# Seven products for eight: the second feed-forward product by Strassen's scheme, with the weights' sums on GpSimd

## The chip, the cores and the metric

The kernel runs on one NeuronCore of a Trainium2 chip. Its time is device microseconds for one execution of the whole program. TensorE (PE) multiplies and writes only into PSUM (eight banks of 128 x 512 float32); VectorE (DVE), ScalarE (ACT) and GpSimd (POOL) work on SBUF; DVE and ACT also read PSUM; SyncE (SP) issues the DMA loads. Each engine runs its own instructions strictly in order, and the engines wait for each other by semaphores.

## The reference

Two decoder blocks on 512 tokens of width 1024, in float32. All that matters here is the end of the second block: the feed-forward layer and the last norm.

```
    h = h + merged @ w_out[l]
    hn = rmsnorm(h, norm2_g[l])
    h = h + jnp.square(jax.nn.relu(hn @ w_ff1[l])) @ w_ff2[l]
return rmsnorm(h, final_g)
```

`w_ff1` is 1024 x 4096 and `w_ff2` is 4096 x 1024.

## The kernel before

**Products in three passes.** A float32 matrix is kept as two float32r parts, `hi` (a rounded copy, made by ACT) and `lo` (the rest, made by a DVE subtraction of two SBUF operands): `split`, line 516. `mm3` (line 559) multiplies hi x hi, hi x lo and lo x hi into one PSUM bank. So each 128 x 128 by 128 x 512 step is three matmuls of 512 columns.

**The feed-forward stage** starts at line 1465. The 4096 hidden columns go by in four quarters (`q`, line 1468), and each quarter has two products:

- The first product makes eight tiles of 128 hidden columns by 512 tokens (`dense_T`, 24 matmuls each). `unit` loads 512 KB of `w_ff1` into a `w_raw` buffer and splits it into one of three `w_hi`/`w_lo` pairs. ACT applies Relu, DVE squares, and `split` writes the tile into `HB` (hi and lo).
- The second product multiplies `HB` (stationary, tokens as columns) by 1024 rows of `w_ff2` (moving), in two halves of 512 output columns: `dense_N`, four units of 24 matmuls per half. That is 8 units and 192 matmuls a quarter. `ev_ff` adds each of the eight result tiles (4 token tiles x 2 column halves) to `x16`, the residual, with one DVE addition that reads PSUM.
- In the last quarter `out_proj` goes by token halves, so that the norm of the first tokens is done while the rest is multiplied. It keeps four of the split units in free places of `KR` and `HA` and loads the other four twice (12 units). Then square (ACT), `rstd` (one small DVE operation and a power on POOL), scaling and the store of a tile.

**The order.** The program is recorded and then laid out by a planner (`Recorder.schedule`, line 198) that works with written-down costs and gives each engine a fixed order, with the more urgent of the ready operations first. It counts an SBUF operation of POOL with two operands at 2.1 ns an element and 100 ns, and it lets no engine slow another. All instructions are issued from line 274, so the profile tells groups apart by their tiles: `bank` is PSUM, `arena` the shared scratch tile, `sp` small column vectors, `sq` the norm's scratch. Buffers are handed out in the order of the program text: a third use of a `w_hi` buffer in turn waits for the matmuls of the first.

Of the kernel before, what the change touches and what calls it, by code (L numbers as in the profile page):

```python
# [29 lines left out]
AF = mybir.ActivationFunctionType  # L30
OP = mybir.AluOpType
# [248 lines left out]
T = 512  # L280
D = 1024
# [126 lines left out]
def body(ctx: ExitStack, tc: tile.TileContext, x, norm_pre_w, norm_post_w, positions, norm1_g, norm2_g, final_g,  # L408
# [4 lines left out]
    v, s, g, pe, sy = (rec.engine(n) for n in ("vector", "scalar", "gpsimd", "tensor", "sync"))  # L413
# [4 lines left out]
    def tiles(n, bufs, name, dt=F32, p=pool):  # L418
        return Ring([p.tile([128, n], dt, name=f"{name}{i}") for i in range(bufs)])

    w_raw, w_hi, w_lo = tiles(1024, 2, "w_raw"), tiles(1024, 3, "w_hi", F32R), tiles(1024, 3, "w_lo", F32R)
    HA = [pool.tile([128, 8, T], F32R, name=f"ha{i}") for i in range(2)]
    HB = [pool.tile([128, 8, T], F32R, name=f"hb{i}") for i in range(2)]
    KR = pool.tile([128, 8, T], F32R, name="kr")
    x16 = pool.tile([128, NT, D], F32, name="x16")
    sqr = tiles(1024, 1, "sq")
    tmp = Ring([sqr.tiles[0][:, i * T:(i + 1) * T] for i in range(2)])
    ar = Arena(pool.tile([128, ARENA], F32, name="arena"), ARENA)
    bank = [pp.tile([128, T], F32, name=f"bank{i}") for i in range(8)]
    dn = Ring(bank[:4])  # L430
# [7 lines left out]
    def small(n=4):  # L438
        return sp_ring(128, n)

    x2 = x[0]
    w_in, w_out, w_in2, w_br_a, w_br_b, w_out2, w_ff1, w_ff2, cmp_w1_k, cmp_w1_v = packed

    def bcast(row, n):
        return bass.AP(tensor=row.tensor, offset=row.offset, ap=[[0, 128], [1, n]])
# [7 lines left out]
    def tt(e, o, a, b, op):  # L453
        e.tensor_tensor(o, a, b, op)
# [4 lines left out]
    def strided(t, off, *dims):  # L459
        return bass.AP(tensor=t.tensor, offset=t.offset + off, ap=[list(t.ap[0])] + [list(d) for d in dims])  # L460
# [5 lines left out]
    def norm_weight(dst, row):  # L466
        sy.dma_start(dst, bcast(row, D))
        return dst[:, :512], dst[:, 512:]
# [37 lines left out]
    def rstd(ss):  # L506
        r = small(1)
        v.scalar_tensor_tensor(r, ss[:, 0:1], EPS, ss[:, 1:2], op0=OP.add, op1=OP.add)
        tt(g, r, r, mhalf[:, :1], OP.pow)
        return r  # L510
# [5 lines left out]
    def split(hi, lo, src, scale=None, e=v):  # L516
        if scale is None:
            s.activation(hi, src, AF.Copy)
            tt(e, lo, src, hi.bitcast(F32), OP.subtract)
        else:  # L520
            s.activation(hi, src, AF.Copy, scale=scale)
            v.scalar_tensor_tensor(lo, src, scale, hi.bitcast(F32), op0=OP.mult, op1=OP.subtract)

    def square(t, c, ss, e=None):

        cs = slice(c * 512, c * 512 + 512)
        if e is not None:
            e.tensor_tensor_reduce(tmp(128, T), x16[:, t, cs], x16[:, t, cs], 1.0 / D, 0.0, OP.mult, OP.add,
                                   ss[:, c:c + 1])
            return  # L530
        s.activation(tmp(128, T), x16[:, t, cs], AF.Square, scale=1.0 / 32, accum_out=ss[:, c:c + 1])
# [27 lines left out]
    def mm3(ps, l, r, lsl, rsl, first, last):  # L559
        for i, (a, b) in enumerate(((0, 0), (0, 1), (1, 0))):  # L560
            pe.matmul(ps, l[a][lsl], r[b][rsl], start=first and i == 0, stop=last and i == 2)
# [16 lines left out]
    def dense_N(w, c0, ncol, H, toks, evac, ready=(), row0=0):  # L578
        nk = 1024 // ncol
        pss = {t: dn(128, ncol) for t in toks}  # L580
        for u, k0 in enumerate(range(0, 8, nk)):
            m = min(nk, 8 - k0)
            wu = ready[u] if u < len(ready) else unit(w, row0 + k0, m, (c0, c0 + ncol))
            for t in toks:
                for k in range(m):
                    mm3(pss[t], H, wu, (ALL, k0 + k, slice(t * 128, t * 128 + 128)), (ALL, k),
                        k0 + k == 0, k0 + k == 7)
        for t in toks:
            evac(t, pss[t])
# [7 lines left out]
    first, raw2 = [], w_raw  # L597
# [4 lines left out]
    for t in range(NT):  # L602
        ss = small(2)
# [390 lines left out]
    def gdn_z(h):  # L994
# [4 lines left out]
    dn, s1, p1 = Ring(bank[:3]), Ring(bank[4:7]), Ring([bank[7], bank[3]])  # L999
    s2, p2 = s1, p1  # L1000
    steps = {"k": gdn_keys, "i": gdn_inverse, "s": gdn_states, "f": gdn_finish, "c": conv, "p": moba_proj,
             "a": moba_pair, "z": moba_z, "g": gdn_z}
# [3 lines left out]
    dn = Ring(bank[:4])  # L1006
# [6 lines left out]
    def places(n):  # L1013

        ps = [(KR[:, 4 * i:4 * i + 2], KR[:, 4 * i + 2:4 * i + 4]) for i in range(2)]
        ps += [[a[:, 4 * i:4 * i + 4, 256:] for a in HA] for i in range(2)]
        ps += [[a[:, 4 * i:4 * i + 4, :256] for a in HA] for i in range(2)]
        return ps[:n]

    def out_proj(w, M, toks, evac, held, room=(), order=(0, 1, 2, 3), early=4, row0=0):  # L1020

        pss = {(cg, t): dn(128, T) for cg in range(2) for t in toks}
        runs = [(cg, us) for us in (order[:early], order[early:]) for cg in range(2) if us]
        todo, room, reuse = 8, list(room), bool(held)
        for n, (cg, us) in enumerate(runs):
            got, steps = {}, [(u, t) for u in us for t in toks]
            if reuse and n == len(runs) - 1 and sum((cg, u) not in held for u in us) < 4:  # L1030
                steps.sort(key=lambda s: s[1])
            for u, t in steps:
                if u not in got:
                    keep = room.pop(0) if todo <= len(room) else None
                    got[u] = held.get((cg, u)) or unit(
                        w, row0 + 2 * u, 2, (cg * 512, (cg + 1) * 512), place=keep)
                    if keep:
                        held[cg, u] = got[u]
                    todo -= 1
                for k in range(2):  # L1040
                    mm3(pss[cg, t], M, got[u], (ALL, 2 * u + k, slice(t * 128, t * 128 + 128)), (ALL, k),
                        u == order[0] and k == 0, u == order[3] and k == 1)
            if us[-1] == order[3]:
                for t in toks:
                    evac(cg, t, pss[cg, t])

    SS = {}
# [18 lines left out]
    held = {}  # L1066
# [301 lines left out]
    dn = Ring(bank[:4] + bank[7:])  # L1368
    dense_T(q0, f0, q1, H=H, parts=2)
    dn = Ring(bank[:4])  # L1370
# [41 lines left out]
    def cmp_values(_):  # L1412
        hv = compress(1, cmp_w1_v)
        for gr in range(2):
# [6 lines left out]
            for i in range(2):  # L1421
# [4 lines left out]
    steps = {"v": dense(1024, 512, ev_hv), "k": dense(2560, 512, ev_kv1), "l": dense(3072, 280, ev_kv2),  # L1426
             "q": dense(2048, 512, ev_q2), "g": hgrn_gates, "s": hgrn_head, "f": hgrn_finish, "p": hgrn_proj,
             "z": lambda h: dense_T(hz(h), H=H), "c": cmp_keys, "d": cmp_values}
# [30 lines left out]
    held = {}  # L1459
# [2 lines left out]
                 early=4 if half else 3)  # L1462


    ar.at = 0
    r_f = ar.ring(T, 4)
    w_fin = norm_weight(ar.take(D), final_g)
    for q in range(4):
        def ff_unit(ci, q=q):
            def ev(ps):  # L1470
                f = r_f(128, T)
                s.activation(f, ps, AF.Relu)
                tt(v, f, f, f, OP.mult)
                split(HB[0][:, ci], HB[1][:, ci], f)
            return w_ff1, q * 1024 + ci * 128, ev

        first = 3 if q == 0 else 0
        if first:
            dense_T(*(ff_unit(ci) for ci in range(first)), H=HA, parts=2)
        for ci in range(first, 8):  # L1480
            dense_T(ff_unit(ci), H=HA)

        def ev_ff(cg, t, ps, q=q):
            cs2 = slice(cg * 512, cg * 512 + 512)
            tt(v, x16[:, t, cs2], x16[:, t, cs2], ps, OP.add)
            if q < 3:
                return
            if cg == 0:
                SS[t] = small(2)
            ss = SS[t]  # L1490
            square(t, cg, ss)
            if cg == 1:
                r = rstd(ss)
                ys = [r_f(128, T) for _ in range(2)]
                tt(v, ys[1], x16[:, t, 512:], w_fin[1], OP.mult)
                v.scalar_tensor_tensor(ys[0], x16[:, t, :512], r, w_fin[0], op0=OP.mult, op1=OP.mult)
                s.activation(ys[1], ys[1], AF.Copy, scale=r)
                for c, y in enumerate(ys):
                    sy.dma_start(out[0, t * 128:(t + 1) * 128, c * 512:c * 512 + 512], y)

        if q < 3:
            for cg in range(2):
                dense_N(w_ff2, cg * 512, 512, HB, range(4), lambda t, ps: ev_ff(cg, t, ps), row0=8 * q)
        else:
            held = {}
            for half in range(2):
                out_proj(w_ff2, HB, (2 * half, 2 * half + 1), ev_ff, held,
                         () if half else places(4), row0=8 * q)

    rec.issue()  # L1510
    return rec
# [30 lines left out]
```

## Time and profile before

| | |
|---|---|
| time, median of 3 runs | 1135.95 us (1135.94 to 1136.45) |
| time of the profiled execution | 1135.46 us |
| its span, first to last instruction | 1133.8 us |
| mean granted TensorE clock over the span | 0.996 of full speed |

The span is what the profile shows instruction by instruction; the 1.7 us between it and the execution's own time lie before the first and after the last instruction. [...]

### The profile page before, as it was taken

How to read it: one execution, taken by the hardware profiler on the slowest of the kernel's cores; microseconds unless marked ns; L12 is line 12 of the kernel's file. 1: busy time of each engine (PE TensorE's matmuls, PEld its weight loads, DVE VectorE, ACT ScalarE, POOL GpSimd, SP SyncE). 2: the span in 40 equal slices, each digit the busy share in tenths (PEclk: the TensorE clock that was granted, in tenths of full speed). 3: DMA queues.
4: the chain of work that ended last, by engine and by line, in shares of the span. 5: the costliest groups of instructions: out<-in, count | busy, mean ns of one | idle time of the engine just before them, and what ended most of it. 6: DMA issues, size and time to landing. Idle time of an engine off the chain costs nothing.

```text
span 1133.8 us, 15260 instructions
## 1 busy us (share of the span) xinstructions
PE 1110.9 (98%) x5808; PEld 920.2 (81%) x5808; DVE 690.5 (61%) x1487; ACT 531.4 (47%) x1003; POOL 40.6 (4%) x65
## 2 busy tenths in 40 slices
PE   8999999999999999999999999999999999999997
PEld 7887888787789877978678778879888888888886
DVE  7585867879676366698966734574533433443463
ACT  4665646476455334466846623353422322422352
POOL 1010101010010000000000000000000000000000
PEclk9999999999999999999999999999999999999999
DMA  5323222222532321234111123252322222222341
GB/s 211 130 86 96 59 85 67 78 67 77 206 113 100 106 78 60 75 130 141 38 57 38 57 93 112 93 186 84 121 94 93 93 101 104 93 93 95 104 154 74
DMA packets 44857, 111.68 MB, mean 99 GB/s; under 512 B 10480, under 2 KB 18032, under 8 KB 44784
## 3 DMA queue, kind: packets, MB, share of 16 engines
q1 hardware_dynamic: 44784, 110.72, 28.8%
q8 instruction: 45, 0.74, 0.3%
q14 instruction: 28, 0.23, 0.1%
HBM read 106.77 MB, written 3.93 MB: 98 GB/s over the span
## 4 chain that ended last, share of the span: by engine, by line
PE 81%; DVE 12%; ACT 3%; DMA 2%; issue 1%; POOL 1%; POOLq 0%; SPq 0%; ACTq 0%; DVEq 0%
PE bank L274 81%; DVE arena L274 7%; DVE w_lo L274 2%; ACT arena L274 1%; DVE kr L274 1%; ACT w_hi L274 1%; DMA w_raw<-in_w_out_dram 1%; DMA arena<-in_w_out_dram 1%; DVE sp L274 1%; POOL sp L274 1%; DMA arena<-in_norm_pre_w_dram 0%; DVE hb L274 0%; ACT kr L274 0%; DVE x L274 0%; ACT sq L274 0%
## 5 line engine op out<-in xcount | busy, mean ns | idle before, releaser
L274 PE MATMUL bank<-ha,w_hi 128*128 128x512 f32 (+1 forms) x1504 | 460.8, 384 | 0.0
L274 PEld LDWEIGHTS bank<-ha,w_hi 128*128 128x128 f32 x1504 | 273.0, 189 | 46.1 <-issue 0.8
L274 PE MATMUL bank<-ha,w_lo 128*128 128x512 f32 (+1 forms) x752 | 287.0, 382 | 0.0
L274 DVE TENSOR_TENSOR w_lo<-w_raw,w_hi 128x1024 fp32r<-128x1024 f32 (+2 forms) x127 | 153.7, 1211 | 181.5 <-ACT w_hi L274 180.9
L274 ACT ACTIVATE w_hi<-w_raw 128x1024 fp32r<-128x1024 f32 (+2 forms) x127 | 133.2, 1050 | 227.7 <-PE bank L274 212.3
L274 PE MATMUL bank<-w_hi,hb 128*128 128x512 f32 x608 | 192.8, 392 | 0.1
L274 PEld LDWEIGHTS bank<-ha,w_lo 128*128 128x128 f32 x752 | 141.8, 189 | 23.2 <-issue 0.3
L274 PEld LDWEIGHTS bank<-w_hi,hb 128*128 128x128 f32 x608 | 114.2, 188 | 24.0 <-DVE x L274 0.5
L274 PE MATMUL bank<-w_lo,hb 128*128 128x512 f32 x304 | 119.0, 391 | 0.5 <-DVE w_lo L274 0.5
L274 ACT ACTIVATE arena<-bank 128x512 f32<-128x512 f32 (+5 forms) x158 | 74.3, 485 | 60.5 <-PE bank L274 57.2
L274 DVE TENSOR_TENSOR w_lo<-arena,w_hi 128x1024 fp32r<-128x1024 f32 (+2 forms) x49 | 59.5, 1214 | 70.6 <-ACT w_hi L274 70.5
L274 PE MATMUL bank<-w_hi,ha 128*128 128x512 f32 (+3 forms) x384 | 98.8, 344 | 2.1 <-ACT w_hi L274 2.1
L274 PE MATMUL bank<-arena 128*128 128x128 f32 (+9 forms) x672 | 96.6, 311 | 1.9 <-DVE arena L274 0.9
L274 ACT ACTIVATE arena<-arena,sp 128x384 f32<-128x384 f32 (+3 forms) x156 | 83.3, 561 | 30.7 <-DVE sp L274 27.9
L274 PEld LDWEIGHTS bank<-arena 128*128 128x128 f32 (+2 forms) x672 | 76.8, 173 | 21.9 <-issue 12.5
L274 ACT ACTIVATE w_hi<-arena 128x1024 fp32r<-128x1024 f32 (+3 forms) x57 | 54.8, 963 | 79.5 <-PE bank L274 75.5
L274 PE MATMUL bank<-ident,arena 128*128 128x128 f32 (+1 forms) x476 | 83.4, 277 | 5.1 <-DVE arena L274 3.4
L274 PE MATMUL bank<-kr,hb 128*128 128x512 f32 (+3 forms) x336 | 82.6, 357 | 2.4 <-DVE sp L274 1.9
L274 PEld LDWEIGHTS bank<-ident,arena 128*128 128x128 f32 (+1 forms) x476 | 58.5, 139 | 25.4 <-DVE arena L274 8.8
L274 PEld LDWEIGHTS bank<-w_hi,ha 128*128 128x128 f32 x384 | 67.5, 193 | 9.7 <-ACT w_hi L274 2.3
L274 PEld LDWEIGHTS bank<-kr,hb 128*128 128x128 f32 x336 | 59.5, 188 | 16.3 <-DVE sp L274 4.6
L274 POOL TENSOR_TENSOR sp<-sp,mhalf 128x1 f32<-128x1 f32 (+1 forms) x36 | 30.6, 850 | 1021.3 <-DVE sp L274 1016.6
(152 smaller groups left out, 1179.5 us busy)
## 6 DMA issues: line engine op xcount, KB each, us to landing
w_raw<-in_w_in_dram SPq DMA_DIRECT2D x62, 512.0 KB, 3.3
w_raw<-in_w_ff_dram SPq DMA_DIRECT2D x45, 512.0 KB, 3.5
arena<-in_w_ff_dram SPq DMA_DIRECT2D x23, 512.0 KB, 3.5
w_raw<-in_w_out_dram SPq DMA_DIRECT2D x17, 512.0 KB, 3.5
arena<-in_w_out_dram SPq DMA_DIRECT2D x9, 512.0 KB, 3.5
x<-in_x_dram SPq DMA_DIRECT2D x8, 512.0 KB, 5.4
arena<-in_w_in_dram SPq DMA_DIRECT2D x8, 512.0 KB, 3.2
arena<-blocks_x SPq DMA_DIRECT2D x8, 256.0 KB, 2.9
```

What stands on the lines that cost most here:

```text
L274: self.issued.append((i, getattr(getattr(self.nc, ops[i].engine), method)(*args, **kw)))
```

## The change

The second product of each quarter is a product of A (512 tokens x 1024 hidden rows) and B (1024 hidden rows x 1024 columns). The change cuts A into token halves and into even and odd row tiles (`r`, the two tiles of a pair `j`), and B into the same rows and two column halves. Each block product is then 256 tokens x 512 rows x 512 columns: 4 pairs x 2 token tiles x 3 passes, 24 matmuls of 512 columns. Strassen's scheme needs seven such products, named by their number in the code: 1, 3, 7, 4, 5, 2, 6 in this order (`seventh`), where eight stood before.

- `WQ` holds a quarter of `w_ff2` unsplit (8 loads of 512 KB, one buffer). For products 1, 3, 7, 4 and 6 POOL adds or subtracts two blocks of it, in two instructions of 1024 columns each, into one of three `r_ws` buffers. Then every product has its weights split in two units of 1024 columns, of 12 matmuls each: 14 units a quarter. Here they are called by product and half: 1a, 1b, 3a, ...
- `sums` runs after every second tile of the first product. DVE makes the sums of A's blocks (256, 256 and 512 columns, and 256 into `A6`), and `split` is done for 256, 512 and 768 columns. They go into `KR` and `HB` (`slot`). The slot of product 6 is that of product 1, written from `A6` once product 1 is through.
- `add_to` adds a product's two PSUM tiles to (or takes them from) `x16`: 10 calls, 20 DVE operations a quarter. Products 7 and 6 go on adding into the banks of 1 and 3, after these were read.
- In the last quarter `finish` does the last norm for tokens 0 to 255 after product 5 and for the others after product 6, which there runs by token tile. Later quarters use banks 4 to 7 for the first product.

```diff
--- before.py
+++ after.py
@@ -1462,16 +1462,82 @@
                  early=4 if half else 3)
     ar.at = 0
-    r_f = ar.ring(T, 4)
     w_fin = norm_weight(ar.take(D), final_g)
+    r_f, r_sum, r_ws = ar.ring(2 * T, 2), ar.ring(4 * 256), ar.ring(2 * T, 3)
+    WQ = ar.take(8 * D).rearrange("p (j r c n) -> p j r c n", j=4, r=2, c=2)
+    A6 = ar.take(D).rearrange("p (j c) -> p j c", j=4)
+    flat = lambda a: a.rearrange("p k t -> p (k t)")
+    two = flat(KR).rearrange("p (x n j c) -> p x n j c", x=2, n=2, j=4)
+    four = [flat(a).rearrange("p (n j c) -> p n j c", n=4, j=4) for a in HB]
+    slot = {3: [two[:, x, 0] for x in range(2)], 4: [two[:, x, 1] for x in range(2)]}
+    slot.update({m: [a[:, n] for a in four] for n, m in enumerate((7, 5, 2, 1))})
+    slot[6] = slot[1]
+    pairs = {1: ((0, 0), (1, 1), OP.add), 3: ((0, 1), (1, 1), OP.subtract), 4: ((1, 0), (0, 0), OP.subtract),
+             6: ((0, 0), (0, 1), OP.add), 7: ((1, 0), (1, 1), OP.add), 2: ((0, 0),), 5: ((1, 1),)}
+    def sums(j, f):
+        sm = r_sum(128, 4, 256)
+        tt(v, sm[:, 3], f[:, 0, 0], f[:, 1, 1], OP.add)
+        split(slot[1][0][:, j], slot[1][1][:, j], sm[:, 3])
+        split(two[:, 0, :, j], two[:, 1, :, j], strided(f, 0, (768, 2), (1, 256)))
+        tt(v, sm[:, 0], f[:, 1, 0], f[:, 1, 1], OP.subtract)
+        tt(v, sm[:, 1:3], f[:, 0], f[:, 1], OP.add)
+        split(four[0][:, :3, j], four[1][:, :3, j], sm[:, :3])
+        tt(v, A6[:, j], f[:, 0, 1], f[:, 0, 0], OP.subtract)
+    def seventh(m, pss, first, last, inner=True):
+        ws = []
+        for js in (slice(0, 2), slice(2, 4)):
+            q = [WQ[:, js, r, c] for r, c in pairs[m][:2 if len(pairs[m]) > 1 else 1]]
+            if len(q) > 1:
+                a = r_ws(128, 2, T)
+                tt(g, a, q[0], q[1], pairs[m][2])
+            else:
+                a = q[0]
+            ws.append((w_hi(128, 2, T), w_lo(128, 2, T)))
+            split(*ws[-1], a)
+        steps = [(j, i) for j in range(4) for i in range(2)]
+        if not inner:
+            steps.sort(key=lambda x: x[1])
+        for j, i in steps:
+            for n, (a, b) in enumerate(((0, 0), (0, 1), (1, 0))):
+                pe.matmul(pss[i], slot[m][a][:, j, i * 128:i * 128 + 128], ws[j // 2][b][:, j % 2],
+                          start=first and j == 0 and n == 0, stop=last and j == 3 and n == 2, skip_group_check=True)
+    def add_to(r, c, pss, op=OP.add):
+        for i in range(2):
+            a = x16[:, 2 * r + i, c * 512:c * 512 + 512]
+            tt(v, a, a, pss[i], op)
+    def finish(t):
+        r = rstd(SS[t])
+        y = r_f(128, 2, T)
+        tt(v, y[:, 1], x16[:, t, 512:], w_fin[1], OP.mult)
+        v.scalar_tensor_tensor(y[:, 0], x16[:, t, :512], r, w_fin[0], op0=OP.mult, op1=OP.mult)
+        s.activation(y[:, 1], y[:, 1], AF.Copy, scale=r)
+        for c in range(2):
+            sy.dma_start(out[0, t * 128:(t + 1) * 128, c * 512:c * 512 + 512], y[:, c])
+    F = {}
     for q in range(4):
+        for k in range(8):
+            sy.dma_start(WQ[:, k // 2, k % 2].rearrange("p c n -> p (c n)"), w_ff2.part(8 * q + k, 1, (0, D)))
         def ff_unit(ci, q=q):
             def ev(ps):
-                f = r_f(128, T)
+                if ci % 2 == 0:
+                    F[q] = r_f(128, 2, 2, 256)
+                f = F[q][:, ci % 2].rearrange("p h c -> p (h c)")
                 s.activation(f, ps, AF.Relu)
                 tt(v, f, f, f, OP.mult)
-                split(HB[0][:, ci], HB[1][:, ci], f)
+                if ci % 2:
+                    sums(ci // 2, F[q])
             return w_ff1, q * 1024 + ci * 128, ev
         first = 3 if q == 0 else 0
@@ -1479,33 +1545,40 @@
             dense_T(*(ff_unit(ci) for ci in range(first)), H=HA, parts=2)
         for ci in range(first, 8):
             dense_T(ff_unit(ci), H=HA)
-        def ev_ff(cg, t, ps, q=q):
-            cs2 = slice(cg * 512, cg * 512 + 512)
-            tt(v, x16[:, t, cs2], x16[:, t, cs2], ps, OP.add)
-            if q < 3:
-                return
-            if cg == 0:
+        dn = Ring(bank[4:])
+        b01, b23, b45, b67 = (bank[i:i + 2] for i in (0, 2, 4, 6))
+        seventh(1, b01, True, False)
+        split(*slot[6], A6)
+        add_to(1, 1, b01)
+        seventh(3, b23, True, False)
+        add_to(0, 1, b23)
+        seventh(7, b01, False, True)
+        add_to(0, 0, b01)
+        seventh(4, b45, True, True)
+        add_to(1, 0, b45)
+        add_to(0, 0, b45)
+        seventh(5, b67, True, True)
+        add_to(0, 0, b67, OP.subtract)
+        add_to(0, 1, b67)
+        if q == 3:
+            for t in range(2):
                 SS[t] = small(2)
-            ss = SS[t]
-            square(t, cg, ss)
-            if cg == 1:
-                r = rstd(ss)
-                ys = [r_f(128, T) for _ in range(2)]
-                tt(v, ys[1], x16[:, t, 512:], w_fin[1], OP.mult)
-                v.scalar_tensor_tensor(ys[0], x16[:, t, :512], r, w_fin[0], op0=OP.mult, op1=OP.mult)
-                s.activation(ys[1], ys[1], AF.Copy, scale=r)
-                for c, y in enumerate(ys):
-                    sy.dma_start(out[0, t * 128:(t + 1) * 128, c * 512:c * 512 + 512], y)
-        if q < 3:
-            for cg in range(2):
-                dense_N(w_ff2, cg * 512, 512, HB, range(4), lambda t, ps: ev_ff(cg, t, ps), row0=8 * q)
-        else:
-            held = {}
-            for half in range(2):
-                out_proj(w_ff2, HB, (2 * half, 2 * half + 1), ev_ff, held,
-                         () if half else places(4), row0=8 * q)
+                for c in range(2):
+                    square(t, c, SS[t])
+                finish(t)
+        seventh(2, b01, True, True)
+        add_to(1, 0, b01)
+        add_to(1, 1, b01, OP.subtract)
+        if q == 3:
+            for t in (2, 3):
+                SS[t] = small(2)
+                square(t, 0, SS[t])
+        seventh(6, b23, False, True, inner=q < 3)
+        add_to(1, 1, b23)
+        if q == 3:
+            for t in (2, 3):
+                square(t, 1, SS[t])
+                finish(t)
     rec.issue()
     return rec
```

## Rows read from the trace of the kernel before

**Rows 1.** the page, busy time by engine, share of the span, instructions

```profile
PE 1110.9 (98%) x5808; PEld 920.2 (81%) x5808; DVE 690.5 (61%) x1487; ACT 531.4 (47%) x1003; POOL 40.6 (4%) x65
```

**Rows 2.** windows, feed-forward stretch: length, busy time by engine, clock, DMA

```profile
782.00:1127.00 345.00, 345.00 (x1575) 287.59 (x1572) 146.38 (x171) 112.40 (x148) 2.08 (x3) 1.00 0.29 100
```

**Rows 3.** the chain of waits from 760 us on: start, length, what

```profile
759.81 361.79 PE bank L274 x1676
...
1129.42 0.75 DVE arena L274
```

**Rows 4.** timeline of PE, end of the last second product: start, length, operation

```profile
1115.98 2.88 PE L274 MATMUL bank<-kr,hb 128*128 128x512 f32 x12
...
1121.42 2.88 PE L274 MATMUL bank<-kr,hb 128*128 128x512 f32 x12
```

**Rows 5.** groups by line and shape, 782 to 1126 us

```profile
L274 DVE TENSOR_TENSOR w_lo<-w_raw,w_hi 128x1024 fp32r<-128x1024 f32 x40 | 49.0, 1225 | 104.5 <-ACT w_hi L274 104.5
L274 ACT ACTIVATE w_hi<-w_raw 128x1024 fp32r<-128x1024 f32 x40 | 42.4, 1061 | 115.5 <-PE bank L274 111.5 <-DMA w_raw<-in_w_ff_dram 2.7 <-ACT hb L274 0.8
...
L274 ACT ACTIVATE arena<-bank 128x512 f32<-128x512 f32 x32 | 18.6, 581 | 0.0
```

**Rows 6.** timeline of DVE, first product and its evacuation

```profile
812.46 1.23 DVE L274 TENSOR_TENSOR w_lo<-w_raw,w_hi 128x1024 fp32r<-128x1024 f32 x1 [2.22 <-ACT w_hi L274]
813.60 0.69 DVE L274 TENSOR_TENSOR arena<-arena 128x512 f32<-128x512 f32 x1
...
841.03 1.28 DVE L274 TENSOR_TENSOR x<-x,bank 128x512 f32<-128x512 f32 x2
```

**Rows 7.** groups by line and shape, whole run, DVE: a 256-wide sum

```profile
L274 DVE TENSOR_TENSOR arena<-arena 128x256 f32<-128x256 f32 x12 | 4.5, 420 | 0.0
```

**Rows 8.** groups by line and shape, whole run, POOL

```profile
L274 POOL TENSOR_SCALAR_AFFINE_SELECT arena<-arena 128x512 f32<-128x512 f32 x6 | 3.8, 637 | 5.8 <-ACT arena L274 5.6
...
L274 POOL TENSOR_SCALAR_AFFINE_SELECT ident<-ones 128x128 f32<-128x128 f32 x1 | 0.3, 282 | 0.1
```

**Rows 9.** timelines of POOL and DVE around 115 and 178 us

```profile
114.88 0.64 POOL L274 TENSOR_SCALAR_AFFINE_SELECT x<-x 128x512 f32<-128x512 f32 x1
...
177.50 0.64 POOL L274 TENSOR_SCALAR_AFFINE_SELECT arena<-arena 128x512 f32<-128x512 f32 x1
...
114.95 1.11 DVE L274 TENSOR_TENSOR x<-arena,gates 128x512 f32<-128x512 f32 x1
...
177.55 0.68 DVE L274 TENSOR_TENSOR arena<-bank,sp 128x512 f32<-128x512 f32 x1
...
178.85 0.68 DVE L274 TENSOR_TENSOR arena<-arena,gates 128x512 f32<-128x512 f32 x1
```

**Rows 10.** timelines of POOL and DVE around 435 us, POOL at 477

```profile
434.73 1.92 POOL L274 TENSOR_TENSOR sp<-sp,mhalf 128x4 f32<-128x4 f32 x1 [85.78 <-DVE sp L274]
477.14 1.01 POOL L274 TENSOR_TENSOR sp<-sp,mhalf 128x4 f32<-128x4 f32 x1 [40.49 <-DVE sp L274]
...
434.56 1.22 DVE L274 TENSOR_TENSOR w_lo<-arena,w_hi 128x1024 fp32r<-128x1024 f32 x1
```

**Rows 11.** timeline after the last matmul

```profile
1127.06 0.69 DVE L274 TENSOR_TENSOR x<-x,bank 128x512 f32<-128x512 f32 x1 [2.33 <-PE bank L274]
...
1129.42 0.75 DVE L274 SCALAR_TENSOR_TENSOR arena<-x,sp,arena 128x512 f32<-128x512 f32 x1 [0.66 <-POOL sp L274]
1130.17 0.81 SPq L274 DMA_DIRECT2D out_dram<-arena  x2
```

**Rows 12.** loads of the feed-forward weights: size each, median us from issue to landing

```profile
w_raw<-in_w_ff_dram SPq DMA_DIRECT2D x45, 512.0 KB, 3.5
arena<-in_w_ff_dram SPq DMA_DIRECT2D x23, 512.0 KB, 3.5
```

## The prediction

> **What bounds the kernel now.** First the page's engine line: TensorE is busy for 98% of the run, DVE for 61%, POOL for 4% [rows 1]. An average over stages doesn't say what this stage is worth, so the next view is the window over the feed-forward stage, 782 to 1127 us: TensorE is busy for all 345.00 us, at the full granted clock, while DVE works 146.38 us and POOL 2.08 us [rows 2]. The chain of waits agrees: from 759.81 us on it is one piece of 361.79 us of matmuls, and only then come DVE, ACT and the power on POOL, of which the last piece starts at 1129.42 us [rows 3]. So whatever takes a matmul out of this stage shortens the run by a matmul, as long as TensorE never has to wait for operands. Nothing else that is removed here is worth anything by itself.
>
> **What is removed.** Two lines of the matmul timeline, 24 matmuls apart, start at 1115.98 and 1121.42 us: 5.44 us for 24, 0.2267 us each [rows 4]. A quarter's second product falls from 192 to 168 matmuls of the same 128 x 512 shape. Over four quarters that is 96 x 0.2267 = **21.76 us**. Four units of weights fewer are loaded too (64 loads of 512 KB, where the rows count 45 and 23 [rows 12]); TensorE never waited for one, so that is worth nothing. A quarter is then 360 matmuls, 81.6 us.
>
> **What DVE has to do now.** Its price for an operation is start to start: the 1024-wide `lo` lasts 1.23 us but the next one starts after 1.14; two additions from PSUM take 1.28 together, so 0.60 each [rows 6]. Taking the same 0.09 off the 256-wide sum's 0.42 gives 0.33 [rows 7], and a 768-wide one lies between, at 0.87. Per quarter: 8 `lo` parts of the first product's weights 9.1, 8 squares 4.8, A's sums and splits four times 0.33 + 0.33 + 0.60 + 0.33 + 0.60 + 0.87 + 0.33 = 3.39, so 13.6, `A6`'s `lo` 1.1, 14 `lo` parts of the second weights 16.0, 20 additions 12.0: together 56.6 of 81.6 us, against 32.6 now. ACT gets 22 weight splits at 1.06, 8 Relus at 0.58 [rows 5] and 7168 columns of A's parts, which is at least 7.4 at the same rate: some 36 us. Both fit, on average. SP issues 16 loads a quarter, as now.
>
> **What POOL has to do.** Ten sums a quarter with two operands of 1024 columns. No row has one. The nearest is a one-operand select: 282 ns for 128 columns and 637 for 512, so 0.92 ns a column and 0.16 us besides [rows 8]. Below, a sum at that rate takes 1.11 us. Above, with each operand read in its turn, 2 x 0.95 + 0.16 = 2.06 us. I take 2.06, because the row's instruction reads one operand and this one reads two. Ten are 21 us of 81.6, so POOL by itself keeps up.
>
> **The wait that the change adds** lies between POOL and DVE. At 114.88 us POOL starts a select; DVE starts a product of two SBUF operands 0.07 later, and it lasts 1.11 us instead of the 0.68 of its twin at 178.85. It ends at 116.06, 0.54 after POOL does (512 columns take about that), so it stood still while POOL read. An addition with an operand in PSUM, started 0.05 after a select at 177.50, took its usual 0.68 [rows 9]. It works the other way as well: the power that takes 1.01 us alone took 1.92 when a 1024-wide `lo` had begun before it [rows 10]. So a sum on POOL and a `lo`, a square or a sum on DVE exclude each other; only DVE's additions from PSUM run beside a sum. Behind a DVE instruction that is held stand the rest of DVE's queue (additions that free banks, the next `lo`), and TensorE waits for these. The planner knows nothing of this.
>
> [...]
>
> **Where it costs.** Take the start of product 1 as zero. A half product is 12 matmuls, 2.72 us. There are three split buffers, so 3a can be split once the last unit of the first product is through (0), 3b at 2.7, 7a at 5.4, 7b at 8.2. The sums have three buffers as well: those for 1a, 1b, 3a, 3b and 7a can be made during the first product, and each later one is released by the split three places before it. So 7b, 4a and 4b start as soon as 3a, 3b and 7a are split, all in the first dozen microseconds, when DVE also ends the first product. Half 7b is needed at 5 x 2.72 = 13.6. By then DVE has to do, in about the order in which things come ready: last square 0.60, sum for slot 1 0.33, 3a 1.14, slot 1 0.33, slot 3 0.60, difference 0.33, 3b 1.14, two sums 0.60, product 1's additions 1.20, 7a 1.14, `A6` 0.33, the 768 columns 0.87, `A6`'s `lo` 1.14, 7b 1.14: 10.9 us. It starts at 0.8 (Relu and hand-overs) and waits some 0.5 for ACT, so without POOL it ends at 12.2, 1.2 early with 0.2 for the hand-over to TensorE. With three sums of 2.06 between, less the 1.2 of additions that run beside one, 5.0 us come on top: 3.8 late. Some of a sum will fall on a moment in which DVE waits anyway, so I take **3.5 us a quarter, 14.0 in all**. With sums of 1.11 it is 1.0 a quarter. Behind 7b the pressure goes: products 5 and 2 need no sums.
>
> [...]
>
> **What I cost at nothing, and its cover.** The step into product 1: from the last tile's end through Relu, square, sum, both parts of the split is about 3.5 us, and the first matmul that needs it is the 19th, 18 x 0.2267 = 4.1 us on; without that cover, or with one sum in the way, up to 1.5 a quarter. Banks: product 7 adds into the banks of product 1 and needs them read, with product 3's 5.4 us between. `WQ`'s single buffer: a row block comes free when the last split or sum that reads it is done, before product 6 ends, and the next quarter has the first product's 43.5 us for eight loads that land in 3.5 us [rows 12]; SP issues in order, so a load that waits holds the `w_raw` loads behind it, but these are two units ahead. Between the sum for tokens 256 to 383 and those for 384 to 511 there are now 12 matmuls instead of 24, so the scaling of the one tile (DVE 0.75) can push the other's addition after the last matmul [rows 11]: 0.3 us on the path.
>
> **The sum.** Against the profiled execution's 1135.46 us: 1135.46 - 21.76 + 14.0 + 0.3 = **1128.0 us**. The median of the runs is 0.5 higher, well within what I can't tell.
>
> **The rivals.**
> - *The sums hide after all.* DVE gets its operations in ahead of POOL, or a sum is nearer to 1.11 us, and every quarter stays within its 1.2 us of lead: 1135.46 - 21.76 + 0.3 = 1114.0, and up to 1119 with about 1 us a quarter. For it: DVE is busy only 70% of a quarter, and no row shows who goes first when both stand waiting. Against it: how POOL's three late sums fall together with DVE's fullest stretch.
> - *The port eats the gain* (the other side). All five sums that fall into the second product (7b, 4a, 4b, 6a, 6b) hold DVE for their whole length: 5 x 2.06 - 1.2 of lead - 1.2 of additions = 7.9 a quarter, 31.6 in all, 1145.6 us. It decides from 21.46 / 4 = 5.4 us a quarter on; below 4.9 the kernel is still faster by more than 0.2%. For it: DVE's work in that stretch, 12 `lo` parts, 20 additions, `A6` and the last tile's 4 us, 30.8 us, plus five sums is 41, and the stretch has 168 x 0.2267 = 38.1. Against it: 6a and 6b are two products ahead of their use, and DVE's last additions may run on into the next first product.
> - *Late weights.* If SP's order makes product 1 wait for `WQ` by a whole product a quarter (5.44), the gain is gone as well: 1135.46 - 21.46 + 21.8 = 1135.8 us. Against it: 43.5 us of cover.
>
> **How the numbers follow.** 0.2% (2.3 us) is about what a measurement of this kernel can tell from no change. The forecast, stalls of about 2 to 4.8 us a quarter, has 0.47 and its own range of 1122 to 1133. Hidden sums have 0.27, the port that eats the gain 0.22, late weights 0.04. Faster: 0.45 of the forecast, 0.27, and 0.02 of late weights, 0.74. No change: 0.02 of the forecast, 0.09 of the port (stalls of 4.9 to 6.0), 0.01 of late weights, 0.12. Slower: 0.14. The range of 8 in 10 must take in both sides: from 1114, where nothing stalls, to 1138, six microseconds a quarter; about 0.03 lies under it and 0.14 above.
>
> **What the changed profile would show.** Right: 1440 matmuls of the feed-forward kind, still 5.44 us for 24; in each quarter a few idle stretches of TensorE in products 3 to 4, put down to `w_lo` of DVE; 1024-wide `lo` operations that last up to 3 us where a POOL sum lies over their start; additions from PSUM that keep 0.68. The hidden rival: TensorE busy throughout, as now. The port rival: idle stretches in every product to 6, DVE without a gap. Late weights: TensorE waiting for `bank`'s weights with DMA as the releaser, at product 1. The prediction is wrong if a sum costs far from 2.06 us, or if DVE and POOL sums overlap freely.

## The result, and the profile after

The changed kernel took **1143.78 us** (median of 4 runs, 1142.22 to 1145.49), the kernel before 1136.2 us in the same runs: a ratio of 1.0066, 95% interval [1.0049, 1.0083]. It is slower, where 1128.0 was forecast, and lies above the range of 1114 to 1138. The profiled execution was the slowest of the four, 1145.49 us with a span of 1143.8, so the ledger below, made from it, is some 1.7 us above the median.

The page's engine line of the changed kernel, and its loads of the feed-forward weights:

```profile
PE 1102.0 (96%) x5712; PEld 907.0 (79%) x5712; DVE 843.7 (74%) x1639; ACT 564.4 (49%) x1043; POOL 155.5 (14%) x105
...
arena<-in_w_ff_dram SPq DMA_DIRECT2D x43, 512.0 KB, 5.5
w_raw<-in_w_ff_dram SPq DMA_DIRECT2D x21, 512.0 KB, 3.5
```

TensorE has 96 instructions fewer than in [rows 1], as the change says, and yet DVE works 153 us more and POOL 115. There are 64 loads, for 68 in [rows 12].

The windows over the last quarter: first product, then second (length, busy time of PE, PEld, DVE, ACT, POOL, granted clock, DMA share, GB/s). In [rows 2] TensorE had no idle time at all.

```profile
1047.21:1090.73 43.52, 43.52 (x193) 36.04 (x192) 31.30 (x40) 17.25 (x24) 7.70 (x4) 1.00 0.16 55
1090.73:1136.35 45.62, 40.88 (x169) 32.17 (x167) 44.99 (x48) 21.70 (x33) 18.22 (x9) 0.96 0.07 24
```

The first product takes 43.52 us for 192 matmuls, 0.2267 each, as in [rows 4]. The second should take 168 x 0.2267 = 38.08 us and takes 45.62, with DVE busy for 44.99 of them. The four second products take 44.58, 45.62, 45.61 and 45.62 us (from the first matmul of one to that of the next stage, the last one to its end): together **29.1 us more than their matmuls**. The first products lose nothing. The whole ledger, by spans: -21.76 for the matmuls, +29.1 here, +2.1 ahead of the stage, +0.5 after the last matmul; the sum is 9.9, and the spans differ by 10.0.

TensorE's waits in the stage (us in all, times, longest), of which before there were none:

```profile
PE bank L274 <- DVE w_lo L274: 10.3, 7, 2.1
PE bank L274 <- ACT hb L274: 7.9, 4, 2.3
```

They stand at the same three places in every quarter; the first quarter lacks the middle one. The timeline of TensorE in the last quarter (start, length, operation, idle time before):

```profile
1097.31 0.50 PE L274 MATMUL bank<-w_hi,hb 128*128 128x512 f32 x1 [1.88 <-ACT hb L274]
...
1105.27 0.50 PE L274 MATMUL bank<-w_lo,hb 128*128 128x512 f32 x1 [0.73 <-DVE w_lo L274]
...
1110.64 0.39 PE L274 MATMUL bank<-w_hi,kr 128*128 128x512 f32 x1
1113.08 0.69 PE L274 MATMUL bank<-w_lo,kr 128*128 128x512 f32 x1 [2.05 <-DVE w_lo L274]
1113.56 1.05 PE L274 MATMUL bank<-w_hi,kr 128*128 128x512 f32 x2
```

The first is product 1's, at its last pair of row tiles: the step that I had costed at nothing. The second is 7a's `lo`, the third 4a's. The timelines of POOL and DVE over them say why:

```profile
1093.77 2.75 POOL L274 TENSOR_TENSOR arena<-arena 128x1024 f32<-128x1024 f32 x1 [1.50 <-DVE w_lo L274]
1098.95 2.51 POOL L274 TENSOR_TENSOR arena<-arena 128x1024 f32<-128x1024 f32 x1 [2.43 <-DVE w_lo L274]
1105.30 6.64 POOL L274 TENSOR_TENSOR arena<-arena 128x1024 f32<-128x1024 f32 x2 [3.83 <-DVE w_lo L274]
...
1093.61 4.13 DVE L274 TENSOR_TENSOR arena<-arena 128x512 f32<-128x512 f32 x4
...
1099.13 2.89 DVE L274 TENSOR_TENSOR kr<-arena,kr 128x512 fp32r<-128x512 f32 x1
...
1104.00 2.35 DVE L274 TENSOR_TENSOR w_lo<-arena,w_hi 128x1024 fp32r<-128x1024 f32 x2
1106.27 3.43 DVE L274 TENSOR_TENSOR hb<-arena,hb 128x1024 fp32r<-128x1024 f32 x1
1109.62 0.67 DVE L274 TENSOR_TENSOR x<-x,bank 128x512 f32<-128x512 f32 x1
1110.22 2.80 DVE L274 TENSOR_TENSOR w_lo<-arena,w_hi 128x1024 fp32r<-128x1024 f32 x1
1112.94 0.67 DVE L274 TENSOR_TENSOR x<-x,bank 128x512 f32<-128x512 f32 x1
1113.54 3.00 DVE L274 TENSOR_TENSOR w_lo<-arena,w_hi 128x1024 fp32r<-128x1024 f32 x1
```

In these stretches DVE has no gap. The last square and three sums, which begin at 1093.61, take 4.13 us, with POOL's sum of 2.75 lying over them; product 1 gets its slot late. 7a's `lo`, the first of the two that begin at 1104.00, ends at 1105.22, and TensorE waits for it until 1105.27. The 512-wide `lo` at 1099.13 takes 2.89 instead of 0.69, `A6`'s at 1106.27 takes 3.43 instead of 1.22, and 4a's `lo` at 1110.22, on which TensorE waits until 1113.08, takes 2.80 instead of 1.22. The additions from PSUM between them keep their 0.67 (679 ns on the mean of all, below). By groups over the stage (busy, mean ns):

```profile
L274 POOL TENSOR_TENSOR arena<-arena 128x1024 f32<-128x1024 f32 x39 | 111.6, 2874 | 222.5 <-DVE w_lo L274 190.5 <-DMA arena<-in_w_ff_dram 30.0 <-DVE sq L274 2.0
...
L274 DVE TENSOR_TENSOR w_lo<-arena,w_hi 128x1024 fp32r<-128x1024 f32 x67 | 97.7, 1467 | 26.9 <-ACT w_hi L274 26.9
...
L274 DVE TENSOR_TENSOR x<-x,bank 128x512 f32<-128x512 f32 x82 | 52.6, 679 | 4.9 <-PE bank L274 4.9
```

A `lo` part lasts 1467 ns on the mean, 1225 in [rows 5], and a sum 2874, of which part is its own wait.

None of these waits is for a sum that came late. There are three sum buffers, so POOL's sums in the last quarter can be told apart by the `lo` that releases each: 7a's starts at 1089.48 and ends at 1092.27, 4a's starts at 1098.95 and ends at 1101.46. TensorE waits for the two units' `lo` until 1105.27 and 1113.08, more than 11 us later, and the chain into product 1 has no sum of POOL in it.

Two sums that nothing held:

```profile
783.38 4.74 POOL L274 TENSOR_TENSOR arena<-arena 128x1024 f32<-128x1024 f32 x2 [2.02 <-DVE sq L274]
```

That is 2.37 us each, above the 2.06 that I had set as the upper end from [rows 8].

### The profile page after: what moved, and what is told of

Its sections match the earlier page's. It is cut to its first block, busy times and chain, and to the rows that moved or that the text cites. A ratio compares the mean times of both kernels' runs of the same rounds, so it can differ in the third digit from the quotient of the medians.

```text
span 1143.8 us, 15328 instructions
## 1 busy us (share of the span) xinstructions
PE 1102.0 (96%) x5712; PEld 907.0 (79%) x5712; DVE 843.7 (74%) x1639; ACT 564.4 (49%) x1043; POOL 155.5 (14%) x105
## 5 line engine op out<-in xcount | busy, mean ns | idle before, releaser
L274 DVE TENSOR_TENSOR w_lo<-w_raw,w_hi 128x1024 fp32r<-128x1024 f32 (+2 forms) x106 | 133.8, 1263 | 102.2 <-ACT w_hi L274 101.6
L274 ACT ACTIVATE w_hi<-w_raw 128x1024 fp32r<-128x1024 f32 (+2 forms) x106 | 111.0, 1048 | 157.3 <-PE bank L274 135.3
L274 ACT ACTIVATE w_hi<-arena 128x1024 fp32r<-128x1024 f32 (+3 forms) x102 | 102.4, 1005 | 143.6 <-PE bank L274 121.5
L274 POOL TENSOR_TENSOR arena<-arena 128x1024 f32<-128x1024 f32 x40 | 114.0, 2862 | 428.2 <-DMA w_raw<-in_w_out_dram 205.7
L274 DVE TENSOR_TENSOR w_lo<-arena,w_hi 128x1024 fp32r<-128x1024 f32 (+2 forms) x94 | 131.8, 1409 | 47.5 <-ACT w_hi L274 47.4
L274 PE MATMUL bank<-w_hi,hb 128*128 128x512 f32 x480 | 156.2, 394 | 9.5 <-ACT hb L274 7.9
L274 PEld LDWEIGHTS bank<-w_hi,hb 128*128 128x128 f32 x480 | 89.9, 188 | 31.1 <-ACT hb L274 9.6
L274 DVE TENSOR_TENSOR arena<-arena 128x512 f32<-128x512 f32 (+8 forms) x200 | 106.1, 557 | 3.5 <-ACT arena L274 1.4
L274 POOL TENSOR_TENSOR sp<-sp,mhalf 128x1 f32<-128x1 f32 (+1 forms) x36 | 31.5, 875 | 488.0 <-DVE sp L274 483.3
L274 PE MATMUL bank<-w_lo,hb 128*128 128x512 f32 x240 | 94.7, 394 | 2.9 <-DVE w_lo L274 2.7
```

The lines of the kernel that those rows point to most:

```text
L274: self.issued.append((i, getattr(getattr(self.nc, ops[i].engine), method)(*args, **kw)))
```

## The experiments

Each run is the changed kernel with one edit (one is the kernel before with one edit); times are medians, each with its ratio to the kernel before in the same runs. "Lost" is what the four second products take beyond 4 x 38.08 us, by the profile.

Three theories are set against each other. By the port theory, DVE stands still while POOL reads (a hold); "port" is only a name for this, and no run shows what the two engines share. By the load theory, DVE has too much work of its own, whoever makes the sums. By the late-sums theory, TensorE waits because a sum arrives late.

| run | time, us | ratio, 95% interval | lost, us |
|---|---|---|---|
| the change | 1143.78 | 1.0066 [1.0049, 1.0083] | 29.1 |
| no sums | 1115.72 | 0.9825 [0.9809, 0.9841] | 0.1 |
| half of each sum | 1119.58 | 0.9858 [0.9844, 0.9873] | 4.1 |
| sums on DVE | 1116.81 | 0.9833 [0.9818, 0.9847] | 2.6 |
| squares on ACT | 1133.83 | 0.9985 [0.9975, 0.9994] | 17.3 |
| sums on DVE, squares on ACT | 1115.18 | 0.9819 [0.9806, 0.9832] | 2.0 |
| planner that knows the port | 1132.32 | 0.9967 [0.9955, 0.9979] | 11.3 |
| the same, squares on ACT | 1127.07 | 0.9923 [0.9906, 0.9939] | 6.7 |
| POOL for products 1 and 3 only | 1118.94 | 0.9849 [0.9835, 0.9862] | 2.5 |
| the kernel before with 36 idle sums | 1137.48 | 1.0016 [1.0007, 1.0025] | |

**No sums.** The question is whether POOL's reading or DVE's own work takes the time.

```diff
-            if len(q) > 1:
+            if False:
                 a = r_ws(128, 2, T)
                 tt(g, a, q[0], q[1], pairs[m][2])
```

> The changed kernel without POOL's 40 sums: each product's weights are split from its first block alone (the sums are left out of the computation; DVE, ACT, TensorE and the loads keep all their instructions). Port theory (DVE is held while POOL reads): DVE is held no more, its 1024-wide lo operations all last 1.22 to 1.23 us, TensorE idles under 1 us a quarter, 1114 to 1118 us. Load theory (DVE has too much to do after each first product, whoever makes the sums): DVE's work is the same, TensorE still loses over 5 us a quarter, 1134 or more. Late-sums theory (TensorE waits because a sum arrives late, not because DVE stands still): also about 1114, so this run parts load from the other two.

It took 1115.72 us, and 0.1 us is lost. With the same work on DVE, the group of `lo` parts is back at its length:

```profile
L274 DVE TENSOR_TENSOR w_lo<-arena,w_hi 128x1024 fp32r<-128x1024 f32 x67 | 81.6, 1223 | 54.3 <-ACT w_hi L274 54.3
```

So DVE's greater work alone (58.8 us in one second product and the first product behind it, 35.1 before) costs nothing that can be seen: the load theory falls, and the forecast of 21.76 us for the matmuls stands.

**Half of each sum.**

```diff
-                tt(g, a, q[0], q[1], pairs[m][2])
+                tt(g, a[:, 0], q[0][:, 0], q[1][:, 0], pairs[m][2])
+                s.activation(a[:, 1], q[0][:, 1], AF.Copy)
```

> The changed kernel with POOL adding only the first 512 columns of each 1024 and ACT copying the first block for the rest (half of each sum is left out). Port theory: a sum holds DVE for 1.2 us instead of 2.4, and what is lost falls by more than half, since 1.2 us a quarter were cover: of 29 us some 8 to 12 stay, 1122 to 1127. Load theory: no change from the changed kernel, 1140 to 1146. Late-sums theory: a sum comes 1.2 us earlier but waits for a copy of 0.63 on ACT, so about a quarter of the loss goes, 1135 to 1139.

1119.58 us: 4.1 us lost of 29.1. The loss falls far more than by half, as the port theory has it and the others don't, and it falls further than I had worked out: a quarter's cover swallowed nearly all of the shorter holds.

**Sums on DVE.**

```diff
-                tt(g, a, q[0], q[1], pairs[m][2])
+                tt(v, a, q[0], q[1], pairs[m][2])
```

> The changed kernel with the same 40 sums made by DVE instead of POOL: 40 x 1.14 = 45.6 us more of DVE's own work, and nobody holds it. Port theory: a sum of 1.14 us in place of a hold of 2.4 us, 36.5 of the second product's 38.1 us, so TensorE loses 1 to 3 us a quarter, 1118 to 1126. Load theory: 11.4 us a quarter more on the engine that is too full, slower than the changed kernel, 1148 to 1160. Late-sums theory: sums stand in DVE's queue and come later than POOL's in part, 1135 to 1145.

1116.81 us, 27 less than the change, with more work on the engine that had been full. That is below the 1118 to 1126 of the port theory, and far from the 1148 to 1160 and the 1135 to 1145 of the two rivals. A sum on DVE is also made sooner than on POOL (1.22 us for 2.37), so against late sums the trace of the change says more than this run. The groups over the stage:

```profile
L274 DVE TENSOR_TENSOR w_lo<-arena,w_hi 128x1024 fp32r<-128x1024 f32 x67 | 81.7, 1225 | 27.0 <-ACT w_hi L274 27.0
...
L274 DVE TENSOR_TENSOR arena<-arena 128x1024 f32<-128x1024 f32 x39 | 47.3, 1222 | 0.0
```

A sum takes DVE 1.22 us where POOL took 2.37, and the `lo` parts are back at 1225 ns on the mean. The third quarter's second product and the last quarter's first, by windows (the later one first):

```profile
1024.22:1067.74 43.52, 43.52 (x193) 36.05 (x192) 32.22 (x45) 17.25 (x24) 0.00 (x0) 1.00 0.14 49
986.07:1024.22 38.15, 38.15 (x169) 31.41 (x168) 37.03 (x45) 17.76 (x19) 0.00 (x0) 1.00 0.38 137
```

TensorE is busy for all of both, with DVE at 37.03 of 38.15 us in the second product; I had worked out 36.5 of 38.1. What is lost, 2.6 us, is nearly all in the last quarter, the most of it in one wait for 7a's `lo`:

```profile
1080.79 0.50 PE L274 MATMUL bank<-w_lo,hb 128*128 128x512 f32 x1 [1.46 <-DVE w_lo L274]
...
1075.09 2.09 DVE L274 TENSOR_TENSOR hb<-arena,hb 128x1024 fp32r<-128x1024 f32 x2
1077.09 2.51 DVE L274 TENSOR_TENSOR x<-x,bank 128x512 f32<-128x512 f32 x4
```

There DVE's fixed order has `A6`'s `lo`, that of the 768 columns and four additions just ahead of 7a's `lo`; in the third quarter only two additions stand there. It isn't the work of the last norm, which DVE begins at 1099.1.

**Squares on ACT.**

```diff
                 s.activation(f, ps, AF.Relu)
-                tt(v, f, f, f, OP.mult)
+                s.activation(f, f, AF.Square)
```

> The changed kernel with the 32 squares of the first product on ACT instead of DVE (4.8 us a quarter off DVE; one link less that a sum can hold in the chain into product 1). Port theory: the wait at product 1 (1.9 to 2.3 us a quarter) shrinks by one 0.6 us operation and perhaps by one hold, the later ones stay: 1134 to 1141. Load theory: DVE is freed by 4.8 of the 7.4 us that a quarter loses, 1124 to 1130.

1133.83 us, just under the 1134 to 1141 of the port theory, and above the 1124 to 1130 of the load theory. The waits of the last quarter:

```profile
1088.41 0.73 PE L274 MATMUL bank<-w_hi,hb 128*128 128x512 f32 x2 [1.85 <-DVE hb L274]
...
1102.62 0.50 PE L274 MATMUL bank<-w_lo,kr 128*128 128x512 f32 x1 [0.27 <-DVE w_lo L274]
```

The wait at product 1 stays (1.85 after 1.88): one operation less in that chain, but a hold is still in it. The later ones nearly vanish here, from 2.8 to 0.3 us (in the first two quarters about 1.6 stay). So 4.8 us a quarter off DVE bring 2.9 us: the holds are as many, but they cost less where DVE has less to do.

**Sums on DVE and squares on ACT**: both edits together, the version that follows from the two.

> Seven products with the sums on DVE and the 32 squares on ACT: the version that the port theory would choose. DVE gets 11.4 us of sums a quarter and loses 4.8, nobody holds it; of the run with the sums on DVE one wait of 1.5 us in the last quarter and some tenths elsewhere are left to win. Port theory: 1114 to 1117 us. If ACT (some 41 of 81.6 us then) gets in the way of the chain into product 1: 1117 to 1121.

1115.18 us, 0.9819 [0.9806, 0.9832] of the kernel before: the fastest of all, and within the spread of the run without any sums.

**A planner that knows the port.** Is it the holds, or only an order that was made without them?

```diff
+            if op.port:
+                clear = max(clear, port["gpsimd" if n == "vector" else "vector"])
             if clear > t:
...
             start[i], free[n] = t, t + op.cost
+            if op.port:
+                port[n] = t + op.cost
```

`op.port` is set for sums on POOL and for DVE operations with two SBUF operands; a sum is costed at 2.37 us.

> The changed kernel with a planner that knows the port: it lets a POOL sum and a DVE operation with two operands in SBUF exclude each other and counts a sum of 1024 columns at 2.37 us; the work is the same. If the port as such is too full (40 sums of 2.4 and DVE's two-operand work, 24 + 44.6 of 81.6 us a quarter, most of it in the second half): 1130 to 1140. If only the order was wrong, because the planner placed urgent operations behind sums that could wait (6a, 6b): 1116 to 1124.

1132.32 us. The order was part of it: 11 us of the 28 between the change and the run without sums. But 11.3 us are lost in the second products and 5.3 in the first ones, which the change had left untouched. With the squares on ACT besides:

> The planner that knows the port, the sums on POOL and the squares on ACT: the best that is known here for sums on POOL. The port then has 24 us of sums and 39.8 of DVE's two-operand work a quarter. If what is lost grows with how full DVE and the port are: some 5 us under the run with the planner alone, 1122 to 1129. If POOL's sums cost a fixed share whatever stands beside them: no better than that run, 1130 to 1134.

1127.07 us, inside the first range. Relief and order help, yet with the sums on POOL it stays 12 us behind the run with sums on DVE and squares on ACT, whose planner doesn't know the port (1115.18).

**POOL for products 1 and 3 only.**

```diff
-                tt(g, a, q[0], q[1], pairs[m][2])
+                tt(g if m in (1, 3) else v, a, q[0], q[1], pairs[m][2])
```

> The sums of products 1 and 3 on POOL (16 sums, which fall into the first product, where DVE has slack), the other 24 on DVE. Port theory: a hold costs only where DVE is full, so next to nothing is lost against all sums on DVE: 1116 to 1120, of which up to 2 us ahead of the feed-forward stage, where the very first sum holds DVE in the changed kernel too. If every POOL sum costs its share wherever it stands (27 us for 40 sums): about 1127.

1118.94 us. In the second products 2.5 us are lost, as with all sums on DVE: these 16 sums cost nothing there. The expectation placed them in the first product, where DVE has slack. In fact three of each later quarter's four start in the last 8 us of the second product before it (855.48, 859.04 and 861.40 us for the second quarter), with DVE busy throughout. What it gets behind there isn't needed at once, and in the first product that follows DVE works only 31.5 of 43.5 us.

The 2.1 us between the two runs lie ahead of the stage: the first second product starts 2.5 us later (825.10 after 822.63 us). Some 0.3 of it stand there already at 712 us, ahead of the first sum. The first sum runs during the projection in front of the stage, and TensorE waits 1.22 us at 755.81 for an addition of DVE, where with all sums on DVE it has no such wait. But the run without any sums also waits there, 0.61 us, so not all of it is the hold. In the change it is much the same; its timelines of POOL and DVE there, where DVE's `lo` took 1.23 us before:

```profile
735.16 2.41 POOL L274 TENSOR_TENSOR arena<-arena 128x1024 f32<-128x1024 f32 x1 [205.74 <-DMA w_raw<-in_w_out_dram]
...
735.89 2.77 DVE L274 TENSOR_TENSOR w_lo<-arena,w_hi 128x1024 fp32r<-128x1024 f32 x1 [0.86 <-ACT w_hi L274]
```

**The kernel before with idle sums.**

```diff
         sy.dma_start(raw, w.part(k0, nk, *cols))
+        if w is w_ff2:
+            tt(g, r_g(128, n), raw, raw, OP.add)
```

> The kernel before with 36 POOL sums of 1024 columns added that nobody uses (one for each unit of second weights, reading the unit just loaded). DVE is held as in the changed kernel, but works 33 of 87 us a quarter and its lo parts are some 8 us ahead of their use. Port theory: the lo operations beside a sum last 2.4 to 3.6 us and the time stays within 0.2%, 1134 to 1138. If a sum on POOL slows TensorE or costs by itself: 1145 or more.

1137.48 us, 1.0016 [1.0007, 1.0025]. Its timelines of POOL and DVE:

```profile
838.88 1.90 POOL L274 TENSOR_TENSOR arena<-w_raw 128x1024 f32<-128x1024 f32 x1 [2.39 <-DMA w_raw<-in_w_ff_dram]
...
838.95 2.91 DVE L274 TENSOR_TENSOR w_lo<-arena,w_hi 128x1024 fp32r<-128x1024 f32 x1 [4.22 <-ACT w_hi L274]
```

POOL reads from 838.88 to 840.78; the `lo` begun 0.07 us later ends at 841.86, so it stood still for about 1.8 us and then took its 1.1. In the first three quarters TensorE doesn't notice: no product takes longer than before. The 36 sums together cost about 1.7 us, and the profile has all of it in the last quarter, most of it in one wait for a `lo`:

```profile
1114.17 0.50 PE L274 MATMUL bank<-w_lo,hb 128*128 128x512 f32 x1 [1.20 <-DVE w_lo L274]
```

The 40 sums in the change cost 28.

## Why the prediction was wrong

- **What is removed** was right: 96 matmuls, 21.76 us. Without sums the kernel takes 19.8 us less than the one before.
- **The wait that the change adds** was right in kind: in these traces a sum on POOL and a DVE operation with two SBUF operands hold each other up, and PSUM additions run on. A `lo` begun beside a sum took 2.80 us for 1.22 in the change and 2.91 in the run with idle sums; a sum took 2874 ns on the mean of the stage, and 2.37 us where nothing held it; the additions kept 679 ns on the mean.
- **Where it costs** is the step that failed, by its size: 3.5 us a quarter were put down, 7.3 were measured (29.1 / 4). The last quarter's 7.54 are 1.88 at product 1, 0.73 at 7a, 2.05 at 4a, 1.7 in a stretch at the lower clock (an estimate, in the last section), and 1.2 in steps too short for the view of waits. At 7b, where the ledger had put the wait, there is none. Four things were missing. A sum takes 2.37 us, not 2.06. The chain into product 1 was costed at nothing with "up to 1.5 a quarter" if a sum fell into it; the sums for 7a and 7b fall around it in every quarter, and it cost 1.9. The ledger ended at half 7b, and the worst wait came after it, at 4a, because `A6`'s `lo` was held as well. And I took a little off for moments in which DVE would wait anyway; it had none.
- **The port eats the gain** was the rival that came nearest, with 0.22: 7.9 us a quarter and 1145.6 us worked out, 7.3 and 1143.8 measured. That the number is so near is partly luck: its sum has neither the wait at product 1 nor the lower clock (1.9 and 1.7 us in the last quarter), and its sign, idle stretches in every product to 6, isn't in the trace, where TensorE waits for nothing behind 4a. What spoke against it, that 6a and 6b are not urgent, didn't help: POOL took them as soon as their buffers were free, in front of DVE's urgent work.
- **The sums hide after all** left open who goes first when both wait. The timelines show it: at 1093.61 DVE runs one operation of its row, and POOL's sum, begun 0.16 later, gets in before the next. There DVE doesn't get ahead by having its queue full.
- **The sum**, 1128.0, was 15.8 us too low; the 0.3 for the tail (0.5 measured) was about right, and nothing stood in it for the 2.1 us ahead of the stage. Of these, 0.4 stand in the trace already at 712 us, ahead of the first sum. After it TensorE waits 1.36 us at 755.10, where the run without sums waits 0.61 and the kernel before doesn't wait. So the first sum's hold accounts for a part; the cause of the rest isn't shown. Late weights: no wait of TensorE was put down to a load.

What stays open: how the 28 us split between the holds of the very operations that TensorE waited for and the backlog that earlier holds left on DVE, and how much the order adds to both. Nearly all of it vanishes once no sum is on POOL; no run takes the parts from each other.

## What to carry to other kernels

A low busy share (POOL's in [rows 1]) doesn't show that an engine is free to be given work: ask first whether its work holds up the engine that stands before the bottleneck. A hold costs next to nothing where what it delays isn't needed soon (36 sums, about 1.7 us; 16 sums, nothing in the second products), and a part of its length where TensorE is about to need it and the neighbour is full (40 sums of 2.37 us cost 28). So count own work plus holds against the stretch in which they fall, up to the last operand that TensorE needs there. Here the nearly full engine did the work itself in half the time (1.22 us a sum for 2.37), and seven products for eight became worth some 20 us.

## What the runs showed of the hardware

**The clock.** Nothing in the prediction allowed for a change of TensorE's granted clock, which the profile gives as a share of full speed. Windows of the third quarter, around its third wait (columns as above):

```profile
1021.70:1023.90 2.20, 0.17 (x1) 0.00 (x0) 2.20 (x2) 1.04 (x1) 1.09 (x1) 1.00 0.61 231
1023.93:1028.00 4.07, 4.07 (x11) 3.21 (x12) 4.07 (x4) 0.00 (x0) 2.37 (x1) 0.58 0.00 0
1030.00:1034.00 4.00, 4.00 (x19) 3.34 (x18) 4.00 (x6) 1.26 (x2) 0.00 (x0) 1.00 0.72 251
```

TensorE had run at the granted 1.00 through two shorter waits of 1.87 and 0.74 us; after the third, 2.06 us by the timeline, in which it did next to nothing for some 2.2, the grant is 0.58 over 4.07 us, and then 1.00 again. By an estimate from these windows that is (1 - 0.58) x 4.07 = 1.7 us. The windows of all four second products have a grant of 0.96, so by the same estimate about 7 of the 29.1 us, 0.04 of 181.43, go in such stretches; the last quarter's timeline shows it as two matmuls taking 1.05 us at 1113.56, where two take 0.73 after a wait in the run with squares on ACT. Not all of that would be won at the full clock: in the last quarter TensorE would have come to 4b's `lo` some 0.7 us before that one, begun at 1113.54, was ready at 1116.54 (an estimate: twelve matmuls of 0.2267 us from 1113.08 on).

That run shows that the fall doesn't follow from the length of the waits alone. Its windows of the first quarter's second product, and of 10 us around the wait at 1088.41 in the last:

```profile
810.00:853.00 43.00, 39.61 (x172) 31.77 (x171) 36.36 (x36) 19.42 (x24) 19.00 (x7) 1.00 0.09 34
1085.00:1090.00 5.00, 3.15 (x12) 2.28 (x12) 5.00 (x5) 2.29 (x4) 2.14 (x1) 0.92 0.01 3
1090.00:1095.00 5.00, 5.00 (x18) 3.93 (x17) 5.00 (x6) 2.69 (x3) 2.79 (x2) 0.74 0.01 2
```

In the first quarter waits of 1.82, 1.06 and 0.51 us within 15 us left the grant at 1.00; in the last, one wait of 1.85 was followed by 0.74 over 5 us. What told the two apart, no run settled. It made no difference to the time: all four second products of that run take 42.4 us, the first two with 1.6 us of later waits, the last two with the lower clock and later waits of only 0.3.

**The price of a sum on POOL** was 2.37 us for two blocks of rows with a stride, and 1.90 us for one contiguous tile added to itself (the run with idle sums). The two differ in the stride and in the number of tiles read; no run takes these apart.
